# Three edits to the order of the feed-forward's first unit: one maker for its token operands, later token sums for the second row pair, weight splits held back longer

## The chip, the cores and the metric

The kernel runs on one core of one Trainium2 chip. The metric is device time in microseconds (us), lower is better. The core has five engines that run their own instruction queues in order and meet only at semaphores: TensorE (PE; its weight loads are listed apart as PEld), VectorE (DVE), ScalarE (ACT), GpSimd (POOL) and SyncE (SP), which here issues nearly all the transfers between HBM and on-chip memory.

## The reference, cut to what matters

One layer of a streaming encoder: a mixing sub-layer (band attention and gated linear attention) and then a gated feed-forward with a causal depthwise convolution of width 3. 2048 prompt tokens and 32 sample tokens are computed in float32. The change touches the feed-forward and the last projection ahead of it:

```python
merged = sigmoid(gate_a) * (ya @ w_br_a) + sigmoid(gate_b) * (yb @ w_br_b)
x = x + gate_m * rmsnorm(merged @ w_out, g_post_mix)
h = rmsnorm(x, g_pre_ffn) * (1.0 + scale_f) + shift_f        # (tokens, 1024)
u = h @ w_up                                                 # (tokens, 2 * 2816)
uu = concat([conv_state, u]); y = b_dw + sum_j w_dw[j] * uu[j:j + t]
a, g = split(y, 2)
out = (gelu(a) * g) @ w_down
```

## The kernel before, in words

**Precision.** Each float32 operand is split into a rounded high part (made by ScalarE, a copy) and a low part, operand minus high part (made by VectorE). A product of two blocks is three matmuls per slice of 128 rows: high x high, high x low, low x high. So a weight block can be used only when ScalarE and then VectorE have split it, and the third matmul of a product is the first that reads the low part of the weights.

**The feed-forward by a seven-product scheme.** The tokens stand in six segments, taken as three pairs (unit 0, 1 and 2 are the up-projection of the three pairs; nine more units are the down-projection). The 1024 rows of `w_up` are halved, and the output columns come in 22 column pairs of 2 x 128 (one of the a half, one of the g half). Column pairs are counted from 1 in this text; in the code the variable `m` or `cur` is one less in unit 0. The 2 x 2 x 2 block product is done with seven products and sums of blocks in place of eight products: weight blocks A11, A12, A21, A22 and sums S1 = A21 + A22, S2 = S1 - A11, S3 = A11 - A21, S4 = A12 - S2; token blocks B11, B21, B22 and sums T1 to T4. `block` (L1959 on) emits one column pair: in the first pair the products A11·B11, S1·T1, S2·T2, S3·T3, A12·B21, S4·B22, and from the second on A11·B11, then A22·T4 *of the pair before*, S2·T2, S1·T1, S3·T3, A12·B21, S4·B22. Each product is 12 matmuls with 128 x 350 outputs.

**Weights, `weights()` and `part()`.** In unit 0 the four blocks of a column pair are fetched from HBM (`raws<-in_w_up_dram`, L1777, 256 KB each) into eight buffers. VectorE makes the four sums (L1781). ScalarE writes a block's high part (L1807) and VectorE its low part (L1812), in the order A11, A12, S2, S1, S3, S4, A22. The sums are also stored for later units (`sW<-raws`, L1815). A split is held back until its data is some ticks old:

```python
while in_order[0] and cur < 5 and tick[0] < born.get((cur, x), -9) + 2:
    yield
```

A tick is one call of `run_due()`, at least six in a column pair. `prod` (L1854 on), which emits a product, drives the weight maker and the ticks on until its weights have been emitted, if they are not there yet.

**Token operands, `load_ops`.** A maker loads a unit's operands (`ht<-h2T` L1527 and L1529 for B blocks, `ht<-hT` L1676 for the T sums, two loads of two row blocks each) and splits them (high L1721 on ScalarE, low L1722 on VectorE). Unit 0 has two makers: one for B11, T2, T1 and T3, run during the last eight output projections, and one for B21, B22 and T4, put in the queue when these projections are done, since its operands lie where the weights of the output projection lay.

**Token sums, `sums(p)`.** The T sums of pair `p` are made ahead on VectorE (16 subtractions L1555), with loads (L1527, L1529) and stores (L1560) on SP; those of the second pair of segments begin at column pair 3 (`m == 2`) of unit 0.

**The other work of a column pair.** ScalarE copies the first product into the second accumulator (`g<-ad` L1979), takes two results aside (`U2` L1992, `P5` L1996), does the third tap of the convolution (L1885) and the GELU (L1912). VectorE adds the results in (L1999, L2007), does the other taps (L1887), the gate product (L1919) and sums of activations for the down-projection (L1899). From the output projection on, the order on all five engines is the order in which the Python code emits the instructions; nothing reorders them.

Of the kernel before, what the change touches and what calls it, by code (L numbers as in the profile page):

```python
# [39 lines left out]
def dap(ap, offset, dims):  # L40
    return bass.AP(tensor=ap.tensor, offset=ap.offset + offset, ap=dims)


def f32(ap):
    return ap.bitcast(F32)
# [13 lines left out]
def encoder_step(ctx: ExitStack, tc: tile.TileContext, I, O):  # L59
# [5 lines left out]
    in_order = [False]  # L65
# [511 lines left out]
    with ExitStack() as st:  # L577
# [218 lines left out]
        for c in range(17):  # L796
            cur, nxt, after, load = chunks[c:c + 4]
# [28 lines left out]
    with ExitStack() as st:  # L826
# [352 lines left out]
        for x, (h, g) in enumerate(units):  # L1179
            cur, nxt, after = us[x:x + 3]  # L1180
# [253 lines left out]
    tick = [0]  # L1434
# [10 lines left out]
    def soon(n, f):  # L1445

        later(n - 1, f) if in_order[0] else f()
# [90 lines left out]
    def h_tile():  # L1538
        hts.append(hts.pop(0))
        return hts[-1].tile([128, 2, W], F32, name="ht", tag="ht", bufs=3 if hts[-1] is fp0 else 1)  # L1540
# [112 lines left out]
    OPS = ("B11", "T2", "T1", "T3", "B21", "B22", "T4")  # L1653
# [5 lines left out]

    pending = []  # L1660
    made_half = [False]

    def load_ops(todo):

        raws = {}

        def load(i):
            u, x, j, n = todo[i]
            p, g = UNITS[u]
            w = WIDTH[u]  # L1670
            raws[i] = r = h_tile()
            if g is None and x in HB:
                k, s = HB[x]
                load_h(r, [(y, 4 * k + j + y, 2 * p + s) for y in range(2)], w)
            elif g is None:
                nc.sync.dma_start(r[:, :, :w], dap(hT, ((4 * p + HT[x]) * 512 + 128 * j) * W,  # L1676
                                                   [[W, 128], [128 * W, 2], [1, w]]))
            elif x in HB:
                k, s = HB[x]
                nc.sync.dma_start(r[:, :n, :w], dap(actD, ((p * MF + 8 * g + 2 * j + k) * 256 + s) * SEG,  # L1680
                                                    [[2 * SEG, 128], [512 * SEG, n], [1, w]]))
            else:
                nc.sync.dma_start(r[:, :n, :w], dap(aT, ((4 * p + HT[x]) * 11 + 4 * g + j) * 128 * SEG,
                                                    [[SEG, 128], [128 * SEG, n], [1, w]]))

        todo = [(u, x, j, min(2, NK[u] - j)) for u, x in todo for j in (0, 2)]
        ahead = [0]
        when = {}

        def more():  # L1690

            while ahead[0] < len(todo) and len(raws) < (2 if pending else 3):
                u, x, j, n = todo[ahead[0]]
                if UNITS[u][1] is None and x in HT and summed.get(UNITS[u][0], -1) < j + 1:
                    break
                load(ahead[0])
                when[ahead[0]] = tick[0]
                ahead[0] += 1

        more()  # L1700
        for _ in range(3 if in_order[0] else 1):
            yield
        for i, (u, x, j, n) in enumerate(todo):
            more()
            if in_order[0] and i % 2 == 0 and i < 4:
                yield
            while i not in when or in_order[0] and tick[0] < when[i] + 3:

                yield
                more()  # L1710
            at = (7 * u + OPS.index(x)) % len(HP)
            while HLIVE.setdefault(at, (u, x)) != (u, x):

                yield
            made_half[0] = True
            hi, lo = HP[at]
            if j:
                soon(1, lambda at=at, u=u, x=x: HO.update({(u, x): HP[at]}))
            w = WIDTH[u]
            hi, lo, r = hi[:, j:j + n, :w], lo[:, j:j + n, :w], raws.pop(i)[:, :n, :w]  # L1720
            nc.scalar.activation(hi, r, AF.Copy)  # L1721
            soon(1, lambda hi=hi, lo=lo, r=r: nc.vector.tensor_sub(lo, r, f32(hi)))  # L1722
            yield
# [22 lines left out]
    def raw(i, n=4):  # L1746
        if i >= NRAW:
            return raws2[:, 512 * (i - NRAW):512 * (i - NRAW) + 128 * n].rearrange("p (k n) -> p k n", n=128)
        return raws_[:, 512 * i:512 * i + 128 * n].rearrange("p (k n) -> p k n", n=128)
# [12 lines left out]
    def weights():  # L1762


        cols = [(u, m) for u in range(len(UNITS)) for m in range(NM[u])]
        fresh = [UNITS[u][0] == 0 for u, m in cols]
        todo = [(c, x) for c in range(len(cols)) for x in (("A21", "A22", "A11", "A12") if fresh[c] else WOPS)]
        at = {}
        born = {}
        cur = -1  # L1770

        def fetch():
            while todo and free and todo[0][0] <= cur + 1:
                c, x = todo.pop(0)
                at[c, x] = i = free.pop(0)
                born[c, x] = tick[0]
                nc.sync.dma_start(raw(i, NK[cols[c][0]]), w_rows(*cols[c], x))  # L1777

        def total(c, eng, op, out, a, b):
            n = NK[cols[c][0]]  # L1780
            getattr(eng, op)(raw(out, n), raw(a, n), raw(b, n))  # L1781

        def total3(c):
            at[c, "S1"] = s1 = free.pop(0)
            s2, a21 = free.pop(0), at.pop((c, "A21"))
            born.update({(c, x): tick[0] + 1 for x in ("S1", "S2", "S3")})
            eng = nc.vector
            a11, a22 = at[c, "A11"], at[c, "A22"]
            total(c, eng, "tensor_add", s1, a21, a22)

            def others():
                total(c, eng, "tensor_sub", s2, s1, a11)
                total(c, eng, "tensor_sub", a21, a11, a21)
                at[c, "S2"], at[c, "S3"] = s2, a21

            soon(1, others)

        def part(c, x, i):
            u, m = cols[c]
            while True:  # L1800
                place = ring((u, m, x))
                if place:
                    break
                yield
            n = NK[u]
            hi, lo = place
            act = nc.scalar.activation(hi[:, :n], raw(i, n), AF.Copy)  # L1807
            if not in_order[0]:
                tc.keep_in_program_order(act)

            def low():
                nc.vector.tensor_sub(lo[:, :n], raw(i, n), f32(hi[:, :n]))  # L1812
                WO[u, m, x] = place
                if fresh[c] and x in SUM:
                    nc.sync.dma_start(w_rows(u, m, x), raw(i, n))  # L1815
                if fresh[c] and x == "A12":

                    def total4():
                        total(c, nc.vector, "tensor_sub", i, i, at[c, "S2"])
                        at[c, "S4"] = i  # L1820

                    soon(1, total4)
                elif fresh[c] and x == "S2":
                    soon(4, lambda: free.append(at.pop((c, "S2"))))
                else:
                    soon(3 if fresh[c] and x in SUM else 1, lambda: free.append(i))

            soon(1, low)

        fetch()  # L1830
        yield
        for cur in range(len(cols)):
            for x in SPLITS if fresh[cur] else WOPS:
                if fresh[cur] and (cur, "S1") not in at and x == SPLITS[0]:
                    while len(free) < 2:
                        yield
                    total3(cur)
                if x == "A22" and cur + 1 < len(cols) and fresh[cur + 1] and len(free) > 1 \
                        and all((cur + 1, y) in at for y in ("A21", "A22", "A11")):
                    total3(cur + 1)  # L1840
                while (cur, x) not in at:
                    fetch()
                    if (cur, x) not in at:
                        yield
                while in_order[0] and cur < 5 and tick[0] < born.get((cur, x), -9) + 2:

                    yield
                i = at[cur, x]
                if not (fresh[cur] and x == "S2"):
                    del at[cur, x]  # L1850
                yield from part(cur, x, i)
                yield
                fetch()

    wq = weights()

    def prod(out, u, m, x, y, first):
# [302 lines left out]
        while pending and next(pending[0], 1) == 1:  # L2160
            pending.pop(0)

    hq = [load_ops([(0, x) for x in OPS[:4]])]

    def hstep():
        while hq and next(hq[0], 1) == 1:
# [21 lines left out]
    psst.close()  # L2188
    psA = pool(ctx, "psA2", bufs=2, space=PSUM)
    psG = pool(ctx, "psG", bufs=2, space=PSUM)  # L2190
    hq.append(load_ops([(0, x) for x in OPS[4:]]))

    work = pX.tile([128, 12 * W], F32, name="work", tag="mhl")
    YA = [work[:, 2 * W * i:2 * W * i + 2 * W].rearrange("p (x w) -> p x w", w=W) for i in range(4)]
# [20 lines left out]

    for u, (p, grp) in enumerate(UNITS):
        for m in range(NM[u]):
            if u == 0 and m == 2:
                sumq.extend([(NBLK - 2, sums(1)), (NBLK, sums(2))])
            if u == 0 and m == 15:  # L2220

# [10 lines left out]
            if u == len(UNITS) - 1 and m == 2:  # L2232

                for i in range(KD):
                    x = h_tile()[:, :, :SEG] if i < 4 else spare.pop(0) if i < 7 \
# [89 lines left out]
```

## Time and profile before

| what | value |
|---|---|
| median of 3 runs | 3138.6 us (3135.17 to 3140.74) |
| the profiled execution | 3133.41 us |
| its span in the trace | 3131.7 us |
| TensorE busy, share of the span | 97% |
| VectorE / ScalarE busy, share of the span | 71% / 53% |
| granted TensorE clock, mean | 0.994 |
| first matmul of unit 0 | at 1727.87 us of the span |

The rows of a timeline have the start and the time that one group of equal instructions took, the engine, the line of the kernel, the operation, what it writes and reads, its shape and count; in brackets stands how long the engine was idle before it, and what ended that. Buffers `hA` and `hB` hold split weights and tokens, `raws` weights and `ht` tokens as loaded, `ad` and `g` are the accumulators of a column pair, `work` its results. Instructions of one engine overlap at their ends, so what an instruction costs its engine is the step from its start to the next start, a little less than its duration.

### The profile page before, as it was taken

Reading aid. Unit: us, or ns where it says so; the run is one execution under the profiler, and the core shown is the slowest. Engines: PE = TensorE matmul, PEld = TensorE weight load, DVE = VectorE, ACT = ScalarE, POOL = GpSimd, SP = SyncE. Lnnn points to the kernel's source line nnn. Section 1 sums busy time; section 2 is a strip of 40 time slices with the busy share of each in tenths; the row PEclk is TensorE's granted clock in tenths of the full one; section 3 lists DMA queues with packets and bytes.
Section 4 is the critical chain, followed back from the end, with each engine's and each line's share of the span. In section 5 each row is a group of like instructions: output and inputs, shape, how many; then the busy total and the mean of one; then the engine's idle time right before and its main releaser. Section 6 shows DMA issues by size and latency. Waiting matters only on the chain. (4 is left out here: it accounts for less than half of the span.)

```text
span 3131.7 us, 56230 instructions
## 1 busy us (share of the span) xinstructions
PE 3031.8 (97%) x19655; PEld 2928.3 (94%) x19655; DVE 2221.9 (71%) x4801; ACT 1662.0 (53%) x3840; POOL 227.0 (7%) x391
## 2 busy tenths in 40 slices
PE   7999999999999999999999999999999999999997
PEld 5999999989999999889999899999999999999997
DVE  6735527774555555665677899998888779897877
ACT  4412225554555555543455555567665556675755
POOL 0002101112111111110000000000000000000001
PEclk9999999999999999999999999999999999999998
DMA  7434434555333433665566676787886667888784
GB/s 229 141 122 143 127 113 131 141 138 145 111 114 111 122 108 107 191 204 182 156 191 212 221 243 211 229 253 229 263 252 202 192 193 242 261 247 277 237 271 147
DMA packets 593858, 580.09 MB, mean 185 GB/s; under 512 B 53283, under 2 KB 521782, under 8 KB 593574
## 3 DMA queue, kind: packets, MB, share of 16 engines
q1 hardware_dynamic: 548086, 526.78, 55.9%
q10 hardware_dynamic: 44432, 47.34, 4.7%
q8 instruction: 155, 2.54, 0.3%
q0 software_dynamic: 1056, 2.38, 0.3%
q14 instruction: 129, 1.06, 0.1%
HBM read 388.68 MB, written 187.65 MB: 184 GB/s over the span
## 5 line engine op out<-in xcount | busy, mean ns | idle before, releaser
L1870 PE MATMUL ad<-hA,hB 128*128 128x350 f32 (+2 forms) x1734 | 301.8, 324 | 5.8 <-ACT work L1996 3.1
L1870 PEld LDWEIGHTS ad<-hA,hB 128*128 128x128 f32 x1734 | 282.4, 189 | 7.8 <-ACT work L1996 4.2
L78 PE MATMUL pm<-hA,wh 128*128 128x416 f32 x768 | 285.1, 371 | 0.0
L80 PE MATMUL pm<-hA,wl 128*128 128x416 f32 x768 | 269.4, 351 | 0.0
L79 PE MATMUL pm<-hA,wh 128*128 128x416 f32 x768 | 269.4, 351 | 0.0
L1812 DVE TENSOR_TENSOR hA<-raws,hA 128x512 fp32r<-128x512 f32 (+1 forms) x367 | 241.8, 667 | 13.0 <-ACT hA L1807 12.7
L1807 ACT ACTIVATE hA<-raws 128x512 fp32r<-128x512 f32 (+1 forms) x367 | 221.9, 617 | 30.1 <-DMA raws<-in_w_up_dram 10.8
L1870 PE MATMUL ad<-hA,hA 128*128 128x348 f32 (+2 forms) x1308 | 225.4, 323 | 2.6 <-ACT work L1996 1.8
L1870 PE MATMUL g<-hA,hB 128*128 128x348 f32 (+2 forms) x1248 | 217.1, 323 | 6.1 <-ACT work L1992 3.2
L1870 PEld LDWEIGHTS ad<-hA,hA 128*128 128x128 f32 x1308 | 211.7, 188 | 3.9 <-ACT work L1996 2.4
L1870 PEld LDWEIGHTS g<-hA,hB 128*128 128x128 f32 x1248 | 202.3, 188 | 8.9 <-ACT work L1992 4.4
L1870 PE MATMUL ad<-hA 128*128 128x350 f32 (+2 forms) x1173 | 205.1, 324 | 4.2 <-DVE hA L1722 4.1
L1870 PEld LDWEIGHTS ad<-hA 128*128 128x128 f32 x1173 | 191.7, 190 | 5.1 <-DVE hA L1722 4.4
L1812 DVE TENSOR_TENSOR hB<-raws,hB 128x512 fp32r<-128x512 f32 (+1 forms) x289 | 190.9, 667 | 6.7 <-ACT hB L1807 6.3
L1807 ACT ACTIVATE hB<-raws 128x512 fp32r<-128x512 f32 (+1 forms) x289 | 175.8, 617 | 27.5 <-DMA raws<-in_w_up_dram 11.8
L69 ACT ACTIVATE pth<-pp 128x256 fp32r<-128x256 f32 (+1 forms) x288 | 106.4, 373 | 138.2 <-PE pp L1015 133.7
L78 PE MATMUL pn<-wh,hA 128*128 128x256 f32 (+1 forms) x624 | 177.7, 285 | 0.0
L72 DVE TENSOR_TENSOR ptl<-pp,pth 128x256 fp32r<-128x256 f32 (+1 forms) x288 | 118.1, 414 | 83.7 <-ACT pth L69 81.0
L79 PE MATMUL pn<-wl,hA 128*128 128x256 f32 (+1 forms) x624 | 176.6, 283 | 0.0
L80 PE MATMUL pn<-wh,hA 128*128 128x256 f32 (+1 forms) x624 | 176.4, 283 | 0.0
L1979 ACT COPY g<-ad 128x348 f32<-128x348 f32 (+2 forms) x102 | 44.3, 434 | 242.0 <-PE ad L1870 159.6
L1870 PE MATMUL g<-hA,hA 128*128 128x350 f32 (+2 forms) x894 | 156.2, 323 | 3.9 <-ACT g L1979 2.3
(511 smaller groups left out, 8368.0 us busy)
## 6 DMA issues: line engine op xcount, KB each, us to landing
raws<-in_w_up_dram SPq DMA_DIRECT2D x220, 256.0 KB, 4.0
raws<-sW SPq DMA_DIRECT2D x176, 256.0 KB, 4.2
sW<-raws SPq DMA_DIRECT2D x88, 256.0 KB, 3.3
raws<-in_w_down_dram SPq DMA_DIRECT2D x80, 256.0 KB, 5.1
wr<-in_w_in_dram SPq DMA_DIRECT2D x72, 256.0 KB, 3.1
sgT<-tx ACTq DMA_DIRECT2D x80, 208.0 KB, 2.3
wa<-in_w_ada_dram SPq DMA_DIRECT2D x64, 256.0 KB, 2.8
keys<-ks SPq DMA_DIRECT2D x128, 128.0 KB, 2.9
```

The costliest lines, as they stand in the source:

```text
L69: i = nc.scalar.activation(hi, src, AF.Copy)
L72: nc.vector.tensor_sub(lo, src, f32(hi))
L78: nc.tensor.matmul(out, ah, bh, start=first and i == 0, stop=False)
L79: nc.tensor.matmul(out, ah, bl, start=False, stop=False)
L80: nc.tensor.matmul(out, al, bh, start=False, stop=last and i == n - 1)
L1807: act = nc.scalar.activation(hi[:, :n], raw(i, n), AF.Copy)
L1812: nc.vector.tensor_sub(lo[:, :n], raw(i, n), f32(hi[:, :n]))
L1870: nc.tensor.matmul(out[:, :w], l_[:, k], r_[:, k, :w], start=first and k == 0 and i == 0, stop=k == n - 1 and i == 2, skip_group_check=True)
L1979: nc.scalar.copy(g[:, 0, :w], ad[:, 0, :w])
```

## The change: what it does

1. The maker that runs during the output projections is given all seven token operands of unit 0; the second maker is gone. A new flag, set where the second maker was queued, keeps the maker from splitting the fifth and later operand (B21, B22, T4) before the output projections are done.
2. The token sums of the second pair of segments (and the queue entry of the third) begin at column pair 7 in place of 3.
3. The splits of weight blocks are held back over the first 9 column pairs in place of 5, and from the fourth pair on until the data is 3 ticks old in place of 2.

```diff
+    wout_done = [False]
...
+            while u == 0 and OPS.index(x) > 3 and not wout_done[0]:
+
+                yield
             at = (7 * u + OPS.index(x)) % len(HP)
...
-                while in_order[0] and cur < 5 and tick[0] < born.get((cur, x), -9) + 2:
+                while in_order[0] and cur < 9 and tick[0] < born.get((cur, x), -9) + (2 if cur < 3 else 3):
...
-    hq = [load_ops([(0, x) for x in OPS[:4]])]
+    hq = [load_ops([(0, x) for x in OPS])]
...
-    hq.append(load_ops([(0, x) for x in OPS[4:]]))
+    wout_done[0] = True
...
-            if u == 0 and m == 2:
+            if u == 0 and m == 6:
                 sumq.extend([(NBLK - 2, sums(1)), (NBLK, sums(2))])
```

No instruction's kind or size changes. Behind the first edit all lines are 1 to 4 higher in the changed kernel (L1807 is L1811, L1979 is L1983, L1885 is L1889 and so on). What moves is shown here at three places. Where rows of one kind follow each other they are counted with x2, x3.

**ScalarE, around the first-product copy of column pair 6.** Before: behind the third tap of the convolution the high parts of A11, of A12 and S2, the GELU, the high parts of S1 and S3 and of S4, and only then the copy, the high part of A22 and the next tap.

```order
L1885 ACTIVATE work<-g,cw 128x2x348
L1807 ACTIVATE hB_611<-raws 128x512
L1807 ACTIVATE hA_102<-raws 128x512 x2
L1912 ACTIVATE work<-work 128x2x348
L1807 ACTIVATE hA_102<-raws 128x512 x2
L1807 ACTIVATE hB_611<-raws 128x512
L1979 COPY g<-ad 128x350
L1807 ACTIVATE hB_611<-raws 128x512
L1885 ACTIVATE work<-ad,cw 128x2x348
L1992 COPY work<-g 128x350
```

With the change: the high part of A11, the copy, the high part of A12, the tap, the high parts of S2, S1 and S3, and behind the next copy and tap those of S4 and A22.

```order
L1811 ACTIVATE hB_611<-raws 128x512
L1983 COPY g<-ad 128x350
L1811 ACTIVATE hA_102<-raws 128x512
L1889 ACTIVATE work<-ad,cw 128x2x348
L1811 ACTIVATE hA_102<-raws 128x512 x3
L1996 COPY work<-g 128x350
L1889 ACTIVATE work<-g,cw 128x2x348
L1811 ACTIVATE hB_611<-raws 128x512 x2
L2000 COPY work<-ad 128x350
```

Six of the seven high parts of column pair 6 have moved from ahead of its copy to behind it. Column pairs 5, 7, 8 and 9 have the same order in the changed kernel.

**VectorE in the same column pair, with the change.** L2011 and L2003 are the two additions of results, L1785 makes a sum of weights, L1816 the low parts: A12 alone, then S2, S1 and S3 (x3), then S4 and A22 (x2), and A11 of the next pair.

```order
L2011 TENSOR_TENSOR ad<-ad,work 128x350
L1816 TENSOR_TENSOR hA_102<-raws,hA_102 128x512
L1891 SCALAR_TENSOR_TENSOR work<-ad,cw,work 128x2x348
L1785 TENSOR_TENSOR raws<-raws 128x512
L1816 TENSOR_TENSOR hA_102<-raws,hA_102 128x512 x3
L1891 SCALAR_TENSOR_TENSOR work<-ad,cw,work 128x2x348
L1891 SCALAR_TENSOR_TENSOR work<-g,cw,work 128x2x348
L1816 TENSOR_TENSOR hB_611<-raws,hB_611 128x512 x2
L2003 TENSOR_TENSOR g<-g,work 128x350
L1891 SCALAR_TENSOR_TENSOR work<-g,cw,work 128x2x348
```

Before, the low parts of A12 and S2 of this pair stand ahead of the addition at L2007, and the tap that reads `ad` stands behind all seven low parts.

**VectorE in column pair 1.** L1722 is the low part of a token operand: the single one at the head belongs to T3, then come two of B21, two of B22 and one of T4. Before:

```order
L1722 TENSOR_TENSOR hA_103<-ht,hA_103 128x700
L1781 TENSOR_TENSOR raws<-raws 128x512
L1999 TENSOR_TENSOR g<-g,work 128x350
L1781 TENSOR_TENSOR raws<-raws 128x512 x2
L1812 TENSOR_TENSOR hB_610<-raws,hB_610 128x512 x2
L1781 TENSOR_TENSOR raws<-raws 128x512
L1722 TENSOR_TENSOR hA_102<-ht,hA_102 128x700 x2
L1812 TENSOR_TENSOR hA_103<-raws,hA_103 128x512 x2
L1722 TENSOR_TENSOR hA_102<-ht,hA_102 128x700 x2
L2007 TENSOR_TENSOR ad<-ad,work 128x350
L1722 TENSOR_TENSOR hA_102<-ht,hA_102 128x700
```

With the change:

```order
L2003 TENSOR_TENSOR g<-g,work 128x350
L1785 TENSOR_TENSOR raws<-raws 128x512 x2
L1816 TENSOR_TENSOR hB_610<-raws,hB_610 128x512
L1726 TENSOR_TENSOR hA_102<-ht,hA_102 128x700
L1816 TENSOR_TENSOR hB_610<-raws,hB_610 128x512
L1785 TENSOR_TENSOR raws<-raws 128x512
L1726 TENSOR_TENSOR hA_102<-ht,hA_102 128x700 x2
L1816 TENSOR_TENSOR hA_103<-raws,hA_103 128x512
L1726 TENSOR_TENSOR hA_102<-ht,hA_102 128x700
L2011 TENSOR_TENSOR ad<-ad,work 128x350
L1816 TENSOR_TENSOR hA_103<-raws,hA_103 128x512
L1816 TENSOR_TENSOR hB_611<-raws,hB_611 128x512
```

The first low part of B21 has moved ahead of one low part of weights and one weight sum. On ScalarE the first high part of T4 has moved the other way, from ahead of the copy of column pair 2 to behind it, with the high part of S4 between the two of T4:

```order
L1983 COPY g<-ad 128x350
L1725 ACTIVATE hA_102<-ht 128x700
L1811 ACTIVATE hA_102<-raws 128x512
L1725 ACTIVATE hA_102<-ht 128x700
L1889 ACTIVATE work<-ad,cw 128x2x348
```

## The prediction, as it was put on record before the changed kernel ran

> **What bounds the kernel now.** I read the page first, then the windows over unit 0, then TensorE's timeline there and what ended its gaps.
>
> ```profile
> span 3131.7 us, 56230 instructions
> ...
> PE 3031.8 (97%) x19655; PEld 2928.3 (94%) x19655; DVE 2221.9 (71%) x4801; ACT 1662.0 (53%) x3840; POOL 227.0 (7%) x391
> ```
>
> TensorE is the bound, so the change, which alters no matmul, can only move TensorE's gaps. Unit 0 has them in its first part:
>
> ```profile
> 1728.00:1850.00 122.00, 110.20 (x659) 106.99 (x658) 107.55 (x172) 66.67 (x116) 0.26 (x4) 0.99 0.75 237
> 1850.00:2024.00 174.00, 173.21 (x1076) 172.87 (x1076) 163.18 (x258) 96.39 (x167) 0.00 (x0) 1.00 0.68 216
> ```
>
> The columns are TensorE, weight loads, VectorE and ScalarE busy, then POOL, clock and DMA. The first 122 us lose 11.8 us of TensorE, the next 174 us 0.8 us. VectorE is 88% and then 94% busy: it has little slack, and where its queue runs late it catches up slowly. The gaps, and three rows that measure the pace:
>
> ```profile
> 1743.20 2.12 PE L1870 MATMUL ad<-hA 128*128 128x350 f32 x6 [4.12 <-DVE hA L1722]
> ...
> 1765.46 2.10 PE L1870 MATMUL g<-hA 128*128 128x350 f32 x12
> ...
> 1778.98 2.26 PE L1870 MATMUL g<-hA,hB 128*128 128x350 f32 x13
> ...
> 1796.25 1.88 PE L1870 MATMUL g<-hA,hB 128*128 128x350 f32 x10 [1.34 <-DVE hB L1812]
> ...
> 1811.71 2.20 PE L1870 MATMUL g<-hA,hA 128*128 128x350 f32 x12 [1.98 <-ACT g L1979]
> ...
> 1833.31 4.12 PE L1870 MATMUL ad<-hA,hB 128*128 128x350 f32 x24 [2.02 <-ACT work L1996]
> ...
> 1866.22 2.10 PE L1870 MATMUL g<-hA 128*128 128x350 f32 x12
> ```
>
> 1765.46, 1778.98 and 1866.22 are the starts of A22·T4 in column pairs 3, 4 and 10. An undisturbed pair takes 1778.98 - 1765.46 = 13.52 us, so a product takes 1.93 us and a matmul 0.16. From pair 4 to pair 10 pass 87.24 us where six pairs need 81.12: the three gaps at 1796, 1811 and 1833 cost 6.1 us in all. What made the last two late is ScalarE, held by a transfer:
>
> ```profile
> 1765.72 0.43 ACT L1979 COPY g<-ad 128x350 f32<-128x350 f32 x1 [1.61 <-PE ad L1870]
> 1766.07 0.64 ACT L1807 ACTIVATE hB<-raws 128x512 fp32r<-128x512 f32 x1
> 1766.60 0.93 ACT L1885 ACTIVATE work<-ad,cw 128x696 f32<-128x696 f32 x1
> ...
> 1806.80 1.16 ACT L1807 ACTIVATE hA<-raws 128x512 fp32r<-128x512 f32 x2 [4.87 <-DMA raws<-in_w_up_dram]
> ...
> 1832.29 0.63 ACT L1807 ACTIVATE hA<-raws 128x512 fp32r<-128x512 f32 x1 [3.85 <-DMA raws<-in_w_up_dram]
> ```
>
> A high part whose block has not landed stops the queue, and the copies that TensorE needs stand behind it. The longer hold removes these stops. The question is what it puts in their place.
>
> **Edit 3, the longer hold: five late columns.** In the changed order, column pairs 5 to 9 make nearly all their splits behind their own first copy. I add up one such pair, with t = 0 at the start of A22·T4, from starts in the rows above and these of VectorE:
>
> ```profile
> 1773.47 0.53 DVE L1999 TENSOR_TENSOR g<-g,work 128x350 f32<-128x350 f32 x1 [0.87 <-ACT work L1912]
> 1773.91 0.94 DVE L1887 SCALAR_TENSOR_TENSOR work<-g,cw,work 128x696 f32<-128x696 f32 x1
> 1774.76 0.51 DVE L1555 TENSOR_TENSOR ht<-ht 128x348 f32<-128x348 f32 x1
> 1775.19 0.94 DVE L1887 SCALAR_TENSOR_TENSOR work<-g,cw,work 128x696 f32<-128x696 f32 x1
> ...
> 1777.26 0.53 DVE L2007 TENSOR_TENSOR ad<-ad,work 128x350 f32<-128x350 f32 x1 [0.70 <-PE ad L1870]
> 1777.70 0.88 DVE L1919 TENSOR_TENSOR work<-work 128x696 f32<-128x696 f32 x1
> 1778.49 0.69 DVE L1812 TENSOR_TENSOR hA<-raws,hA 128x512 fp32r<-128x512 f32 x1
> ...
> 1780.12 0.69 DVE L1781 TENSOR_TENSOR raws<-raws 128x512 f32<-128x512 f32 x1
> 1780.72 2.50 DVE L1812 TENSOR_TENSOR hA<-raws,hA 128x512 fp32r<-128x512 f32 x4
> ...
> 1795.52 1.28 DVE L1812 TENSOR_TENSOR hB<-raws,hB 128x512 fp32r<-128x512 f32 x2
> ```
>
> Steps from start to start: L1999 0.44, a tap L1887 0.85, a half sum L1555 (or L1899, the same size) 0.43, L1919 0.79, a weight sum 0.60, a low part 0.60 ((2.50 - 0.69) / 3). From the start of a low part to the matmul that waits for it: 1796.25 - 1795.52 = 0.73.
>
> ScalarE: the copy starts at 1765.72 - 1765.46 = 0.26, the high part of A12 at 0.61, the tap at 1.14, and it ends at 1.14 + 0.93 = 2.07. VectorE: the low part of A12, then the tap that reads this result, from 2.10; the weight sum S4 at 2.95, the low part of S2 at 3.55. The matmul that reads it runs at 3.55 + 0.73 = 4.28. TensorE wants it as the third of S2·T2, at 1.93 + 0.32 = 2.25. **Gap 2.03 us.** A12·B21 then starts at 4 x 1.93 + 2.03 = 9.75, and L1999, which waits for the product before it, 0.26 later at 10.01. Behind it stand a tap, a sum, L1919 and two sums, 3.88 us with L1999 itself, then the low part of A11 of the next pair at 13.89, used at 14.62. TensorE wants it at 6 x 1.93 + 2.03 + 0.32 = 13.93. **Gap 0.69 us.** The next t = 0 is 10 matmuls on, at 16.2: a pair costs 16.2 in place of 13.52, so 2.7 us more. Pairs 6, 7 and 8 have one more 0.43 us step (L1899 or L1555) on the way to A11: 3.1 each. In pair 9 three L1555 and three L1899 stand ahead of the low part of S2, 0.3 later than above, 3.0. And A11 of pair 5 is late already: L1999 at 7.98, then L1999, tap, sum, L1899, tap and two sums, 4.37, and 0.73, used at 13.08 where 11.90 was wanted: 1.2.
>
> Sum over pairs 4 to 10: 1.2 + 2.7 + 3 x 3.1 + 3.0 = **16.2 us, where the kernel before loses 6.1: +10.1**. The transfers play no part: the block of A12 is asked for when the low part of A22 has freed its buffer, about 7 us ahead of use.
>
> From pair 10 on the hold is off, and the order of pairs 9 and 10 of the changed kernel turns into that of pairs 5 and 6 of the one before, where the two transfer stops were. At pair 10 TensorE is itself 2 to 3 us later and I count no gap; at pair 11 the same queue of SP (token loads, a store, then A12) stands ahead of the same high part, so I count the 2.02 us again: **+2.0**. Bounds: low, only ScalarE's chain counts (high part of S2 from 1.96 to 2.60, low part, gap 1.1, five times 5.5, no gap at A11, none at pair 11): 5.5 - 6.1 = -0.6. High, both stops return: 16.2 + 4.0 - 6.1 = +14.1. I take +12.1, since the gap at 1796.25 is the same chain, a low part of S2 behind sums in a full VectorE queue.
>
> **Edit 1, one maker: hardly anything.** The gap of 4.12 us at B21:
>
> ```profile
> 1738.70 0.53 DVE L1999 TENSOR_TENSOR g<-g,work 128x350 f32<-128x350 f32 x1 [0.64 <-ACT hA L1721]
> 1739.14 1.28 DVE L1781 TENSOR_TENSOR raws<-raws 128x512 f32<-128x512 f32 x2
> 1740.34 1.29 DVE L1812 TENSOR_TENSOR hB<-raws,hB 128x512 fp32r<-128x512 f32 x2
> 1741.66 0.69 DVE L1781 TENSOR_TENSOR raws<-raws 128x512 f32<-128x512 f32 x1
> 1742.27 1.68 DVE L1722 TENSOR_TENSOR hA<-ht,hA 128x700 fp32r<-128x700 f32 x2
> ...
> 1746.33 0.79 ACT L1721 ACTIVATE hA<-ht 128x700 fp32r<-128x700 f32 x1 [3.98 <-DMA ht<-hT]
> ...
> 1750.86 0.43 ACT L1979 COPY g<-ad 128x350 f32<-128x350 f32 x1 [3.22 <-PE g L1977]
> 1751.21 0.79 ACT L1721 ACTIVATE hA<-ht 128x700 fp32r<-128x700 f32 x1
> ...
> 1753.88 2.10 PE L1870 MATMUL g<-hA 128*128 128x350 f32 x12
> ```
>
> The first low part of B21 passes one low part and one sum: it starts 0.60 + 0.60 = 1.2 us earlier, about 1741.0, and the gap is 2.9 in place of 4.12. After the long gap the clock fell:
>
> ```profile
> 1744.00:1746.00 2.00, 2.00 (x9) 0.50 0.85 228
> ```
>
> Half clock over some 11 matmuls cost about 1.4 us. The Trainium skill, "TensorE: Matmul & The Clock Gate" (the HAM clock gate), says that an idle window of about 3.4 us halves the clock; by it a gap of 2.9 would keep full clock, and the 4.12 here agrees. Without that rule the 1.4 us stay. Either way B22's low parts (four more steps behind B21's first) and then T4 catch TensorE: T4's first high part, at 1746.33 ahead of the copy before, now comes behind the copy. With A11 of pair 2 done 1.4 us earlier, the copy starts at about 49.5 (1749.5), T4's first half at 49.8, the high part of S4 at 50.5, T4's second at 51.0 in place of 51.21. So S2·T2 starts 0.1 to 0.2 before its 1753.88. **-0.1**; bounds 0 and -2.6 (1.2 + 1.4 with nothing late behind it).
>
> **Edit 2, later sums: nothing by itself.** 16 steps of 0.43 us, 6.9 us of VectorE, leave pairs 3 to 8 and go to pairs 7 to 12, with their loads and stores on SP. Pairs 3 and 4 show no gap before. In pairs 7 to 9 they are in the sum above; in 10 to 12 VectorE has them on top of about 12.5 us of work in 13.52, with splits a column ahead as cover, as pairs 6 to 8 have before. Unit 1, which needs them, makes its operands from pair 19 on. If that cover is gone they cost at most their 0.43 each in three pairs, some 3 us.
>
> **Sum.** -0.1 + 10.1 + 2.0 = +12.0 us. The rest of the feed-forward gets another order too (the buffers' turn is shifted); its gaps are many and small, the largest group being
>
> ```profile
> PE g L1870 <- ACT work L1992: 4.3, 5, 1.4
> ```
>
> so I give this +-4 us and no sign. The profiled execution took 3133.4 us, 1.7 more than its span; the changed one would take 3145.4. The median of the runs before is 5.2 above the profiled one, so I put it at 3138.6 + 12.0 = **3150.6 us**.
>
> **Rivals.**
> *The splits come in time (faster).* If VectorE ran ahead so that the low part of S2 ended by 2.25, the three gaps vanish and edit 1 gives its full 2.6: 3138.6 - 6.1 - 2.6 = 3129.9. For it speaks that the stops by transfers are real, 4.87 and 3.85 us; against it that the low part of S2 waits for the tap, the tap for ScalarE, and ScalarE for a copy of the same pair, whatever is idle. Decided by one row: S2's low part in pairs 5 to 9.
> *The gaps trade (no change).* ScalarE's chain alone, with the stops gone: -0.6 to +5, about 3141. It needs the tap and the sum not to delay the low part, against the order of the queue.
> *The clock falls as well (slower still).* Two gaps a pair, 2.0 and 0.7 us, five pairs; a fall of 1.4 us at each first gap would add 7: 3157.6. Against it, the 1.98 us gap at 1811 was followed by no fall.
> *The change doesn't do what it says*: the hold could run out unused; but the order shown is what runs.
>
> **How the numbers follow.** The forecast (slower by 7 to 17 us) 0.70, slower still 0.05, no change 0.17, faster 0.08. A difference of 0.2%, 6.3 us, is about what a measurement here can tell. Slower by more: 0.75; within: 0.17; faster: 0.08. The likeliest case alone spans 3145 to 3156; with the no-change case and the later gaps the range is 3135 to 3158.
>
> **What would show it.** Right: in pairs 5 to 9 a gap of about 2 us ahead of the third matmul of S2·T2, released by VectorE L1816, and one below 1.2 at A11; pairs of 16 to 17 us; no ScalarE wait for `in_w_up` there; a gap released by L2000 near pair 11; B21's gap near 2.9 and a T4 gap grown to some 2.5. Wrong: pairs 5 to 9 at 13.5 us, or the gaps released by a transfer.

## The result, and the profile after

| | before | changed |
|---|---|---|
| median of six runs | 3137.72 us (3135.17 to 3140.74) | 3156.28 us (3149.18 to 3160.48) |
| ratio, 95% interval | | 1.0058 (1.0048 to 1.0068) |
| profiled execution | 3133.41 us | 3160.48 us |
| first matmul of the feed-forward | 1727.87 us | 1736.44 us |
| from there to the end of the span | 1403.8 us | 1422.4 us |

The change is slower by 0.58%, 18.6 us between the medians. The forecast was 3150.6 us, 12.0 slower, in a range of 3135 to 3158. The two profiled executions lie 27 us apart, but 8.6 of that is there when the feed-forward starts, and ahead of that point the engines get the same instructions in the same order. In the profiles of this study that start wanders from 1726.1 to 1736.4 us. So below I count from the first matmul of the feed-forward; there the two profiles differ by 18.5 us, about as the medians do. With one profile of each kernel that is partly luck.

The page of the changed kernel: the same 19655 matmuls are busy for 12.0 us longer, and the rest of the 27 us is waiting.

```profile
span 3158.8 us, 56239 instructions
...
PE 3043.8 (96%) x19655; PEld 2937.5 (93%) x19655; DVE 2223.6 (70%) x4801; ACT 1659.9 (53%) x3840; POOL 226.8 (7%) x391
```

The 12.0 us are the clock. Leaving out the last microseconds of the kernel, the changed kernel's trace has twelve steps of 3.41 us at clock 0.50 and the one before has five; seven more at half rate are 11.9 us. Six of the twelve and three of the five lie ahead of the feed-forward, which is part of the 8.6 us.

TensorE's timeline in unit 0, with the rows that answer to those of the prediction (the first matmul is at 1736.44): B21 and T4 in the first pairs, A22·T4 of pairs 4, 5, 8 and 10, the gaps of pairs 5 and 8, and pair 11.

```profile
1750.44 1.64 PE L1874 MATMUL ad<-hA 128*128 128x350 f32 x6 [3.12 <-DVE hA L1726]
1752.57 1.83 PE L1874 MATMUL ad<-hA 128*128 128x350 f32 x5 [0.49 <-DVE hA L1726]
...
1759.82 0.42 PE L1874 MATMUL g<-hA,hB 128*128 128x350 f32 x1 [1.23 <-ACT hA L1725]
1760.75 3.22 PE L1874 MATMUL g<-hA,hB 128*128 128x350 f32 x11 [0.50 <-DVE hA L1726]
1763.77 2.51 PE L1874 MATMUL g<-hA 128*128 128x350 f32 x12
...
1789.28 4.03 PE L1874 MATMUL g<-hA,hB 128*128 128x350 f32 x24
...
1802.40 1.88 PE L1874 MATMUL ad<-hA,hB 128*128 128x350 f32 x10 [1.05 <-DVE hB L1816]
...
1855.96 2.11 PE L1874 MATMUL g<-hA 128*128 128x350 f32 x12
1858.58 0.59 PE L1874 MATMUL g<-hA,hA 128*128 128x350 f32 x2 [0.51 <-ACT hA L1811]
1860.24 1.88 PE L1874 MATMUL g<-hA,hA 128*128 128x350 f32 x10 [1.08 <-DVE hA L1816]
...
1872.88 2.11 PE L1874 MATMUL g<-hA,hB 128*128 128x350 f32 x12
...
1891.07 2.10 PE L1874 MATMUL g<-hA 128*128 128x350 f32 x12
...
1914.24 3.36 PE L1874 MATMUL ad<-hA,hB 128*128 128x350 f32 x12 [1.76 <-ACT work L2000]
```

Every pair from 5 to 9 has the same three waits: the low part of A11 (1.05 us in pair 5, 0.57 in pair 6, 1.00 in the others), then the high and the low part of S2 (0.51 and 1.08 in pair 8). Pair 8 costs 1872.88 - 1855.96 = 16.92 us in place of 13.52. ScalarE and VectorE in pair 8 show the chain that the prediction added up:

```profile
1856.20 0.43 ACT L1983 COPY g<-ad 128x350 f32<-128x350 f32 x1 [7.10 <-PE ad L1874]
1856.55 0.63 ACT L1811 ACTIVATE hA<-raws 128x512 fp32r<-128x512 f32 x1
1857.08 0.93 ACT L1889 ACTIVATE work<-ad,cw 128x696 f32<-128x696 f32 x1
```

```profile
1857.22 0.69 DVE L1816 TENSOR_TENSOR hA<-raws,hA 128x512 fp32r<-128x512 f32 x1 [1.74 <-ACT hA L1811]
1858.04 0.94 DVE L1891 SCALAR_TENSOR_TENSOR work<-ad,cw,work 128x696 f32<-128x696 f32 x1
1858.90 0.69 DVE L1785 TENSOR_TENSOR raws<-raws 128x512 f32<-128x512 f32 x1
1859.50 0.69 DVE L1816 TENSOR_TENSOR hA<-raws,hA 128x512 fp32r<-128x512 f32 x1
```

ScalarE waits 7.10 us for TensorE, then the copy lets A12's high part through; VectorE does A12's low part, a tap, the sum S4, and only then the low part of S2. Nothing there waits for a transfer.

What was not counted is the clock. Windows of 3.41 us over the changed kernel (columns as in the prediction; the clock stands ahead of the last two):

```profile
1757.86:1761.27 3.41, 1.69 (x9) 1.08 (x8) 1.79 (x4) 2.64 (x5) 0.00 (x0) 1.00 0.47 157
1761.27:1764.68 3.41, 3.41 (x14) 3.26 (x13) 3.38 (x6) 1.03 (x2) 0.00 (x0) 0.50 0.26 77
1805.64:1809.05 3.41, 1.82 (x10) 1.24 (x9) 3.28 (x6) 2.08 (x4) 0.00 (x0) 1.00 1.00 373
1809.05:1812.46 3.41, 3.41 (x14) 3.41 (x13) 1.36 (x2) 1.26 (x3) 0.00 (x0) 0.50 0.46 174
...
1839.78:1843.19 3.41, 1.97 (x11) 1.38 (x9) 2.75 (x4) 2.87 (x5) 0.00 (x0) 1.00 1.05 312
1856.84:1860.25 3.41, 1.82 (x11) 1.24 (x9) 2.90 (x5) 2.72 (x5) 0.00 (x0) 1.00 1.04 335
1873.92:1877.33 3.41, 1.66 (x9) 1.07 (x7) 3.40 (x7) 2.56 (x5) 0.00 (x0) 1.00 1.07 365
1877.33:1880.74 3.41, 3.37 (x11) 3.37 (x12) 2.04 (x3) 0.05 (x1) 0.00 (x0) 0.50 1.06 380
1911.47:1914.88 3.41, 1.65 (x11) 1.36 (x10) 3.13 (x6) 1.66 (x3) 0.00 (x0) 1.00 1.09 307
1914.88:1918.29 3.41, 3.41 (x14) 3.41 (x13) 3.41 (x7) 2.89 (x6) 0.00 (x0) 0.50 0.95 327
...
1800.00:1900.00 100.00, 86.68 (x495) 82.04 (x494) 82.51 (x133) 44.76 (x81) 0.00 (x0) 0.97 0.66 208
```

Behind a stretch in which TensorE was busy for about half the time (1.65 to 1.82 us here) or less, the next 3.41 us may run at clock 0.50, which costs up to 1.7 us. The changed kernel has five such stretches in unit 0 (a fifth at 1751.04, behind B21's gap), the one before has one. Four more cost at most 4 x 1.7 = 6.8 us. The last row, over all five pairs, has a mean clock of 0.97: the two stretches at 1809 and 1877 (2 x 3.41 us at half rate in 100 us) and no other.

The account, from the first matmul of the feed-forward:

| | forecast | measured | how |
|---|---|---|---|
| up to A22·T4 of pair 4 | -0.1 | +1.7 | 52.84 us after the first matmul, 51.11 before |
| pair 4 to pair 10 | +10.1 | +14.6 | 1891.07 - 1789.28 = 101.79, less 87.24 |
| pair 11 to the end of unit 0's gaps | +2.0 | +3.6 | a matmul in pair 14 starts 19.9 later, less 16.3 |
| later | 0 (±4) | -1.4 | 18.5 less 19.9 |
| sum | +12.0 | +18.5 | |

### The profile page after: what moved, and what is told of

It is laid out like the page before. It is cut to its first block, busy times and chain, and to the rows that moved or that the text cites. A ratio compares the mean times of both kernels' runs of the same rounds, so it can differ in the third digit from the quotient of the medians.

```text
span 3158.8 us, 56239 instructions
## 1 busy us (share of the span) xinstructions
PE 3043.8 (96%) x19655; PEld 2937.5 (93%) x19655; DVE 2223.6 (70%) x4801; ACT 1659.9 (53%) x3840; POOL 226.8 (7%) x391
## 5 line engine op out<-in xcount | busy, mean ns | idle before, releaser
L1816 DVE TENSOR_TENSOR hA<-raws,hA 128x512 fp32r<-128x512 f32 (+1 forms) x367 | 243.4, 669 | 15.1 <-ACT hA L1811 14.9
L1811 ACT ACTIVATE hA<-raws 128x512 fp32r<-128x512 f32 (+1 forms) x367 | 223.1, 616 | 17.6 <-PE ad L1874 5.3
L1874 PE MATMUL g<-hA,hB 128*128 128x350 f32 (+2 forms) x1230 | 216.4, 326 | 7.1 <-DVE hB L1816 2.1
L1816 DVE TENSOR_TENSOR hB<-raws,hB 128x512 fp32r<-128x512 f32 (+1 forms) x289 | 191.0, 668 | 7.2 <-ACT hB L1811 6.9
L1811 ACT ACTIVATE hB<-raws 128x512 fp32r<-128x512 f32 (+1 forms) x289 | 175.6, 617 | 30.1 <-DMA raws<-in_w_up_dram 12.1
L1983 ACT COPY g<-ad 128x348 f32<-128x348 f32 (+2 forms) x102 | 44.4, 435 | 253.0 <-PE ad L1874 157.8
```

Source lines behind the costliest of these rows:

```text
L1874: nc.tensor.matmul(out[:, :w], l_[:, k], r_[:, k, :w], start=first and k == 0 and i == 0, stop=k == n - 1 and i == 2, skip_group_check=True)
L1983: nc.scalar.copy(g[:, 0, :w], ad[:, 0, :w])
```

## The experiments

Twelve kernels. The ratio is to the kernel before as it ran beside them (medians of 3137.7 to 3139.1 us). In the last column stands how much later (or sooner) than in the kernel before the 1082nd matmul of the feed-forward (in pair 14) starts in the one profiled execution, counted from the first matmul of each; the matmuls that e4 adds are not counted.

| label | what is in it | median us | ratio (95%) | to pair 14 |
|---|---|---|---|---|
| e12 | edit 1 | 3141.47 | 1.0016 (1.0007 to 1.0025) | +3.1 |
| e6 | edit 2 | 3136.02 | 0.9995 (0.9986 to 1.0004) | +0.9 |
| e1 | edit 3 | 3152.28 | 1.0040 (1.0028 to 1.0053) | +15.0 |
| e2 | edits 1, 2 | 3140.03 | 1.0004 (0.9994 to 1.0013) | +2.4 |
| e5 | edits 1, 3 | 3151.92 | 1.0044 (1.0032 to 1.0057) | +16.3 |
| changed | edits 1, 2, 3 | 3156.28 | 1.0058 (1.0048 to 1.0068) | +19.9 |
| e7 | changed, three steps for five columns | 3143.83 | 1.0020 (1.0011 to 1.0028) | +10.1 |
| e8 | changed, two steps for nine columns | 3147.45 | 1.0030 (1.0019 to 1.0041) | +12.6 |
| e3 | changed, S2 split ahead of A12 | 3174.24 | 1.0111 (1.0098 to 1.0125) | +37.3 |
| e4 | changed, gaps filled with matmuls | 3153.44 | 1.0048 (1.0036 to 1.0061) | +15.6 |
| e9 | before, sums' loads on GpSimd's queue | 3137.24 | 0.9998 (0.9989 to 1.0007) | -2.6 |
| e10 | edit 2, the same | 3137.38 | 0.9999 (0.9990 to 1.0008) | -0.7 |
| e11 | e10, token low parts first | 3144.90 | 1.0020 (1.0011 to 1.0028) | +5.3 |

**Which edit.** Edit 3 alone, on the kernel before:

```diff
-while in_order[0] and cur < 5 and tick[0] < born.get((cur, x), -9) + 2:
+while in_order[0] and cur < 9 and tick[0] < born.get((cur, x), -9) + (2 if cur < 3 else 3):
```

> The kernel before with edit 3 alone (hold for nine columns, three steps from column 3 on). Theory, the hold makes the low part of S2 and of A11 late in column pairs 5 to 9: 12 to 20 us slower than before, gaps released by the low part of S2 (L1812) in all five pairs, pairs of 16.5 to 18 us; somewhat worse than the whole change in these pairs, since here four token sums (0.43 us each) stand in VectorE's queue in pairs 3 to 8. Rival, the three edits share the loss: under 9 us slower.

Measured 1.0040, 13 us, with S2's low part late in all five pairs. TensorE's timeline of pairs 5 and 9 in it:

```profile
1800.37 3.29 PE L1870 MATMUL g<-hA,hB 128*128 128x350 f32 x10 [1.98 <-DVE hB L1812]
...
1869.28 0.90 PE L1870 MATMUL g<-hA 128*128 128x350 f32 x4 [1.07 <-DVE hA L1812]
```

The token sums make pair 5 worse (1.98 in place of 1.08), as expected; over pairs 4 to 10 it is not worse than the changed kernel (101.13 us, 101.79 there), since only one stretch at clock 0.50 falls into them. The changed kernel with the old hold line put back:

> The changed kernel without edit 3: one maker and the later token sums, with the hold of the kernel before. Theory: -3 to +2 us against before, no gap at the low part of S2 in four of the pairs 5 to 9 since the splits run a column ahead again. Rival, the token sums or the maker are what makes the splits late: 5 to 12 us slower than before.

1.0004: the loss goes with edit 3. Edit 2 alone, and the changed kernel without it:

```diff
-if u == 0 and m == 2:
+if u == 0 and m == 6:
```

> The kernel before with edit 2 alone. Theory: the two transfer stops at pairs 6 and 7 get shorter, since SP has no token loads there (up to 3 us gained), and one stop of about 2 us comes at pair 11, with or without a stretch at clock 0.50 (1.7 us): -2 to +2 us against before. Rival, the sums cost VectorE time in pairs 10 to 12 as well: 3 us slower.

> The changed kernel without edit 2: one maker and the longer hold, the token sums from column pair 3 as before. In the changed kernel ScalarE stands 3.59 us at 1913 on a block of w_up, behind eight token loads and a store of the token sums on SP. Theory, this stop is edit 2's: it is gone here, 2 to 4 us faster than the changed kernel, near the hold alone: 3150 to 3154. Rival, the stop comes from the end of the hold, wherever the sums stand: within 1 us of the changed kernel, with the stop at pair 11.

Edit 2 alone is no change that can be told from none. Without it the changed kernel goes from 1.0058 to 1.0044; those intervals overlap, but the profiles differ as the theory said. First the changed kernel's SP ahead of the gap at 1914.24, then its ScalarE there, then ScalarE at the same place with edits 1 and 2, then the window of pairs 10 to 14 with edits 1 and 3:

```profile
1902.26 2.97 SPq L1529 DMA_DIRECT2D ht<-h2T  x4
...
1907.49 1.98 SPq L1781 DMA_DIRECT2D raws<-in_w_up_dram  x2
```

```profile
1913.22 0.63 ACT L1811 ACTIVATE hB<-raws 128x512 fp32r<-128x512 f32 x1 [3.59 <-DMA raws<-in_w_up_dram]
```

```profile
1891.12 0.63 ACT L1811 ACTIVATE hB<-raws 128x512 fp32r<-128x512 f32 x1 [3.62 <-DMA raws<-in_w_up_dram]
```

```profile
1885.00:1945.00 60.00, 60.00 (x374) 60.00 (x374) 57.26 (x91) 33.56 (x60) 0.00 (x0) 1.00 0.72 224
```

The stop at pair 11 is there with the late sums, hold or no hold, and not without them. It is edit 2's. On the kernel before, edit 2 pays for it at the two stops of pairs 6 and 7 (TensorE waits 0.57 us in place of 1.98 in pair 6, not at all in pair 7, 1.00 in pair 8); with the hold those stops are gone anyway, and only the price is left.

Edit 1 alone:

> The kernel before with edit 1 alone. Theory, from the runs with and without it: B21's gap falls from 4.12 to 3.12 us but a second one of 0.4 to 0.9 comes in the same product, and T4's first high part, now behind the copy, makes the wait there 1.23 us in place of 0.27: about 1.5 us slower through column pair 2, the two transfer stops of pairs 6 and 7 as before: 0 to +3 us against before. Rival, the prediction's: -0.1 us through column pair 2.

1.0016: slower, by 3.4 us between the medians, just above what I put down; the interval (0.07 to 0.25%, 2 to 8 us) doesn't exclude it. TensorE's gaps in it at B21 and at T4:

```profile
1748.01 2.12 PE L1874 MATMUL ad<-hA 128*128 128x350 f32 x6 [3.13 <-DVE hA L1726]
...
1757.94 0.42 PE L1874 MATMUL g<-hA,hB 128*128 128x350 f32 x1 [1.23 <-ACT hA L1725]
```

B21's gap falls from 4.12 to 3.13, and T4's first high part comes late by 1.23 (in the kernel that has edit 2 alone it was in time, and the second was late by 0.27). The gap at the transfer stop of pair 6 is 2.52 in place of 1.98, that of pair 7 0.35 in place of 2.02. No second gap followed within B21's product here, though in the changed kernel (0.49) it did.

**How much hold.** The line of edit 3 with one of its two numbers put back:

```diff
 e7: cur < 5 and tick[0] < born.get((cur, x), -9) + (2 if cur < 3 else 3)
 e8: cur < 9 and tick[0] < born.get((cur, x), -9) + 2
```

> The changed kernel, its hold of three steps ended after five columns as before. Theory, each column held costs its own late pair (some 3.4 us with both gaps): only pair 5 is late, 3 to 5 us slower than without edit 3 (3140), 3142 to 3146. Rival, three steps put the splits behind for good and VectorE, nearly full, doesn't catch up: pairs 6 to 9 late too, 3150 or more.

> The changed kernel, its hold of nine columns with two steps throughout. Theory, with two steps the high parts of A12 and S2 stand ahead of the copy in some of the columns and behind it in others (pair 9 as in the changed kernel, pairs 5 and 8 nearly without a gap): 3 to 8 us slower than without edit 3, 3143 to 3148. Rival, the number of columns alone counts: as slow as the changed kernel, 3155.

Both came out as the theory had it, 3143.83 and 3147.45. In e7 only pair 5 has the wait for S2, and the stop by a transfer is back in pair 7:

```profile
1798.77 2.82 PE L1874 MATMUL g<-hA,hB 128*128 128x350 f32 x10 [1.08 <-DVE hB L1816]
...
1835.77 5.69 PE L1874 MATMUL ad<-hA,hB 128*128 128x350 f32 x24 [1.86 <-ACT work L2000]
```

So once the hold ends the splits do get ahead again: VectorE catches up within a pair. In e8 only some of the gaps stood where I had named them: pair 5 is nearly free (0.48 at S2) and pair 9 is late, but pair 8 isn't free. Pairs 7 and 8 wait 1.05 at A11 and little at S2, and pair 9 waits 3.33 at A11, in a profiled execution that was the slowest of its nine (3154.74).

**Is it S2's place in the queue?** In the columns of pairs 5 to 9, S2 ahead of A12; `spent` gives S2's buffer back three steps after the later of its low part and the sum S4:

```diff
-for x in SPLITS if fresh[cur] else WOPS:
+for x in (("A11", "S2", "A12", "S1", "S3", "S4", "A22") if 3 < cur < 9 else SPLITS) if fresh[cur] else WOPS:
...
-    soon(4, lambda: free.append(at.pop((c, "S2"))))
+    spent(c)
```

> The changed kernel, but in the columns of pairs 5 to 9 S2 is split ahead of A12 (the buffer of S2 is given back when both are done). Everything else of the hold stays. Theory, S2's place in the queue behind A12's low part, a tap and the sum S4 makes the gap: its low part then waits for one tap only, some 1.2 us sooner, the loss at S2*T2 falls from 2.0 to 0.9 us a pair, 5 to 6 us faster than the changed kernel and up to 3 more if fewer stretches at clock 0.50 follow: 3147 to 3152. Rival, VectorE's work per pair sets the pace and the gap only moves to A11 or A12*B21: within 1.5 us of the changed kernel.

A miss, and a large one: 18 us slower than the changed kernel. TensorE and ScalarE in pair 8:

```profile
1870.53 0.58 PE L1882 MATMUL ad<-hA,hB 128*128 128x350 f32 x2 [1.64 <-ACT hB L1818]
```

```profile
1864.30 0.63 ACT L1818 ACTIVATE hA<-raws 128x512 fp32r<-128x512 f32 x1
1868.98 0.45 ACT L2004 COPY work<-g 128x350 f32<-128x350 f32 x1 [3.04 <-PE g L1882]
1869.33 0.63 ACT L1818 ACTIVATE hA<-raws 128x512 fp32r<-128x512 f32 x1
```

S2 is a sum and is made late, so its hold runs longest; put first, it holds A12, S1 and S3 as well. They now stand behind the copy of S2·T2's result (1868.98), so S1·T1 waits 1.64 us for its high part, and A11 is late behind it. S2's own low part came hardly sooner: on VectorE two taps now stand ahead of it, and it starts 3.16 us behind the first-product copy in place of 3.30. So the place of S2 alone is not the price. The pair loses at each copy that held splits fall behind; that this is so in general is argued from this one run, in which three stretches at clock 0.50 between 1818 and 1853 us add to the loss.

**Is it the clock?** The changed kernel with matmuls that compute nothing wanted in its gaps, written to the half of `ad` that S1·T1 overwrites:

```diff
+fill = 3 if spare is not None and x == "S2" else 0
...
+if spare is not None and k == 0 and i == 2:
+    fill = 7 if x == "S2" else 3
+for _ in range(fill):
+    nc.tensor.matmul(spare[:, :w], hi[:, 0, :128], hi[:, 0, :w], start=True, stop=True, skip_group_check=True)
```

> The changed kernel with matmuls that compute nothing wanted put into its gaps in pairs 5 to 9: three ahead of S2*T2, seven ahead of its third matmul, three ahead of the third matmul of A11*B11, 0.16 us each, into a half of the buffer that is overwritten later. The queues of the other engines are untouched, so each low part lands when it did. If the two stretches at clock 0.50 that pairs 5 and 9 show cost 1.7 us each and come from the idle time ahead of them, they are gone and the kernel is about 3 us faster than the changed one. Rival, these stretches are hidden by the next late operand: no difference. Third, the gaps are shorter than the added matmuls: up to 3 us slower.

The waits for A11's low part at pairs 8 and 9, and the window over all five pairs:

```profile
1848.67 1.89 PE L1881 MATMUL ad<-hA,hA 128*128 128x350 f32 x10 [0.53 <-DVE hA L1816]
1865.58 1.88 PE L1881 MATMUL ad<-hA,hB 128*128 128x350 f32 x10 [0.52 <-DVE hB L1816]
```

```profile
1795.00:1900.00 105.00, 102.34 (x613) 97.91 (x612) 90.52 (x147) 48.22 (x86) 0.00 (x0) 1.00 0.69 216
```

A pair still takes 16.91 us, so the low parts land when they did, and the clock stays at 1.00. From pair 4 to pair 10 pass 98.79 us in place of 101.79, and the 3.0 us are all in pairs 5 and 9 (16.50 and 16.69 us in place of 18.01 and 18.19): a stretch costs 1.5 us there. The median is 2.8 us lower than the changed kernel's, though the intervals overlap (1.0048 and 1.0058). The profile ends 5.3 us sooner, since no stretch comes at pair 11 either, which the added matmuls don't reach. Of the rivals, "hidden by the next operand" predicts neither. The price of a stretch is what the profiles show; the times alone don't prove it.

**Can it be better than before?** Three tries. First the loads of the token sums on another queue, on the kernel before and on edit 2:

```diff
-load_h(x, [(0, j, 2 * p), (1, j, 2 * p + 1)], w)
+load_h(x, [(0, j, 2 * p), (1, j, 2 * p + 1)], w, nc.gpsimd if p else nc.sync)
```

> The kernel before, its token loads for the sums of the second and third pair issued on GpSimd's queue in place of SP's; nothing else. Theory, the transfer stops of pairs 6 and 7 (1.98 and 2.02 us) come from these loads standing ahead of the blocks of w_up on SP: both gaps are gone, 3 to 5 us faster than before. Rival, the blocks are late by the bandwidth that all transfers share: the gaps stay, within 2 us of before.

> Edit 2 alone (token sums from column pair 7 on) with the loads of the sums on GpSimd's queue. Theory, the gap of 2.23 us at pair 11, and with it the stretch at clock 0.50, are gone: 2 to 4 us faster than edit 2 alone, 3132 to 3135. Rival, shared bandwidth: the gap stays, 3136.

Both within the noise of the kernel before, so both theories miss the time. In e10 the gap at pair 11 does fall, from 2.23 to 0.46 us, and no stretch at clock 0.50 follows it; but two such steps in place of one come behind B21's gap, and pair 8 waits 1.40 us. ScalarE's stops in e9 and what is left of them on TensorE, both now in pair 6:

```profile
1808.96 1.16 ACT L1807 ACTIVATE hA<-raws 128x512 fp32r<-128x512 f32 x2 [2.69 <-DMA raws<-in_w_up_dram]
...
1820.65 0.63 ACT L1807 ACTIVATE hB<-raws 128x512 fp32r<-128x512 f32 x1 [2.78 <-DMA raws<-in_w_up_dram]
```

```profile
1814.66 2.20 PE L1870 MATMUL g<-hA,hA 128*128 128x350 f32 x12 [0.58 <-ACT g L1979]
...
1821.68 2.20 PE L1870 MATMUL ad<-hA 128*128 128x350 f32 x12 [0.95 <-ACT work L1996]
```

The stops shrink from 4.87 and 3.85 to 2.69 and 2.78, and the gaps from 2.0 to 0.6 and 1.0; so SP's queue is about half of it: counted from the first matmul, the blocks behind the first stop are issued at 71.82 us in place of 74.25, 2.4 us sooner, and that stop is 2.2 us shorter. What the rest is made of isn't shown. The 2.6 us gained up to pair 14 are less than the time can show. Then, on top of e10, the token operands' low parts right behind their high parts, and no weight split in two steps of the first pair:

```diff
+if u == 0 and OPS.index(x) > 3:
+    nc.vector.tensor_sub(lo, r, f32(hi))
```

> The kernel before it (edit 2, loads on GpSimd's queue), and in the first column pair two steps take no weight split, and the low parts of B21, B22 and T4 are issued right behind their high parts, so that on ScalarE and VectorE they stand ahead of the next column's three sums and low parts. Theory, the gap of 4.1 us at A12*B21 is VectorE's queue, not the load: it falls to 1 us or less, no stretch at clock 0.50 follows, and some of it comes back at S4*B22, the next A11 and T4: 3 to 5 us faster than without this, 3128 to 3132. Rival, B21's load lands late, or T4's does: the gap moves there, within 1.5 us.

```profile
1742.94 2.04 PE L1873 MATMUL ad<-hA 128*128 128x350 f32 x11 [1.32 <-DVE hA L1723]
1748.34 2.12 PE L1873 MATMUL ad<-hA,hB 128*128 128x350 f32 x6 [1.97 <-DVE hA L1723]
...
1812.68 2.87 PE L1873 MATMUL ad<-hA,hB 128*128 128x350 f32 x10 [2.89 <-DVE hB L1815]
```

B21's gap was VectorE's queue: 4.12 became 1.32. But B22 took 1.97, a stretch at clock 0.50 came all the same, and A11 came late in pairs 4, 5 and 6 (0.62, 1.05 and 2.89), where e10 has no such wait; that this is the price of the splits put off is likely, not shown. 3144.90, 1.0020: slower, where 3128 to 3132 was expected. Of the kernels run, none is shown to be faster than the one before.

## Why the prediction was right, and where it was not

**Right: the direction, the edit and the chain.** Against t = 0 at 1855.96 the copy starts at 0.24 (0.26 forecast), the tap on ScalarE at 1.12 (1.14), the tap on VectorE at 2.08 (2.10), the sum at 2.94 (2.95), the low part of S2 at 3.54 (3.55) and the matmul that needs it at 4.28 (4.28). The 2.03 us forecast ahead of that matmul are there, but in two waits: 0.51 for the high part of S2, ahead of the product, and 1.08 for its low part. The pair takes 16.92 where 16.6 was added up. The gaps are released by L1816 or, for the high part, by L1811, none by a transfer, and e1, e2 and e7 tie them to the hold, a late pair for each column held.

**Too small: the clock.** The forecast for the gaps of pairs 4 to 10 was 16.2 us. Measured are 101.79 - 81.12 = 20.7, of which two stretches at 0.50, in pairs 5 and 9, make 3.0 (e4): without them 17.7. The stretches behind T4 and at pair 11 are two more that the kernel before doesn't have. The step that failed is the one that set aside the rival "the clock falls as well", with a chance of 0.05, because one gap of 1.98 us was followed by no fall. The rival's price of 3157.6 was nearer to the 3156.28 measured than the forecast, though it put a fall into each of the five pairs; the measured 18.6 us lie in the range, but above the likeliest case (7 to 17 us). That row was no bound. The 3.41 us that most of the gap falls into, in the kernel before:

```profile
1808.02:1811.43 3.41, 1.71 (x11) 1.41 (x9) 3.41 (x7) 2.41 (x5) 0.00 (x0) 1.00 0.61 211
```

TensorE was busy for 1.71 us of them. In the changed kernel such steps with 1.65 to 1.82 us were followed by a fall, so it was a near case. What decides, as far as the records show, is not one gap but how busy TensorE was over a stretch, and in pairs 5 and 9 the two waits at S2, 0.51 and 1.1 to 1.3 us, fall into one. The rule of the Trainium skill, "TensorE: Matmul & The Clock Gate" (the HAM clock gate), as I had put it (a gap of 2.9 us keeps full clock) does not hold here: behind B21's gap of 3.12 us the clock fell (1751.04), and the stretch at 1757.86 had waits of 1.23 and 0.50 us and the clock fell behind it.

**Wrong: edit 1.** Forecast -0.1, with a gap of 2.9 at B21 and a T4 that follows in time. B21's gap was 3.12, near enough, but 0.49 more came in the same product, the clock fell as before, and T4's first high part, behind the copy now, was 1.23 us late. S2·T2 starts 27.33 us after the first matmul in place of 26.01: +1.3. The failed step is "With A11 of pair 2 done 1.4 us earlier, the copy starts at about 49.5 (1749.5)". That copy in the changed kernel:

```profile
1758.63 0.43 ACT L1983 COPY g<-ad 128x350 f32<-128x350 f32 x1 [7.20 <-PE g L1981]
```

Counted from the first matmul it stood at 22.99 us before, was forecast at 21.63 and starts at 22.19: 0.8 us sooner, not 1.4. A22·T4 then starts at 23.38, 0.6 later than before, and the stretch at 1761.27 falls into it. e12 puts the edit alone at 1.0016.

**Right for another reason: pair 11.** A gap of 2.0 was counted at the place where one of 1.76 came, released by L2000, with "token loads, a store, then A12" on SP. I booked it to the end of the hold. e2 and e5 show that it belongs to edit 2, which the prediction had as "nothing by itself". That is so alone (0.9995), and not beside edit 3.

**The no-change and the faster case** needed the low part of S2 by 2.25; it starts at 3.54 in pair 8. The gain from the transfer stops was real (TensorE waits for none in pairs 5 to 9), but it was 4.5 of the 6.1 us, since the gap at 1796.25 was never one of them; against it stand 20.7.

## What to carry to other kernels

Where a queue in order feeds the bound engine, holding work back so that it won't wait for a transfer can put it behind the next instruction that waits for the bound engine's own result, as here; price the hold by that copy, once for each column held, and not by the transfer it avoids. Add up a late chain from the rows of one tile in time order, step by step: here it met the measured starts up to S2 within 0.02 us, and the pair within 0.3. Then look at the busy share of the bound engine over each stretch of a few microseconds, since several short waits together can cost it its clock.

## What the hardware showed that was not expected

In the records of the changed kernel every stretch at clock 0.50 in unit 0 lasts 3.41 us, and their starts (1751.04, 1761.27, 1809.05, 1877.33, 1914.88) lie whole multiples of 3.413 us apart (3, 14, 20 and 11). In other profiles a stretch lasts two such steps, 6.83 us (e7 and e12, behind B21's gap). The clock so seems to be decided on a fixed grid of time, by how busy TensorE was in the step before. In the windows above, steps with 1.65, 1.66 and 1.69 us of matmul were followed by half clock, the one with 1.97 was not, and of two with 1.82 one was. The fourteen profiles of this study together say the same. Of the steps of the feed-forward that ran at full clock (the last 20 us left out), all 40 with at most 1.51 us of matmul were followed by half clock, 15 of the 54 with 1.52 to 2.03 us, and none of the 5469 with more. What decides between 1.52 and 2.03 is open; the profile's ends of matmuls are modelled. So equal gaps in five pairs cost a stretch in two of them only, by where they fall on the grid; that is argued from these rows, not tried. It would also let the same program lose 1.5 us or so here or there from run to run. The six runs of the changed kernel fit that: the two with a mean clock of 0.993 took 3149.18 and 3151.41 us, the four with 0.990 or 0.991 took 3155.96 to 3160.48.
